# A two-layer trunk on one core: weights in 8 KB pieces, evenly spaced row passes, attention on the full array

## The chip, the core and the metric

The kernel runs on one core of a Trainium2 chip. The core has TensorE (PE in the profile, PEld its weight loads), VectorE (DVE), ScalarE (ACT), GpSimd (POOL) and SyncE (SP); here SP only issues DMAs, and 16 DMA engines move the data from the chip's memory into the core's. The metric is the time of one execution on the device in microseconds (us). The clock that TensorE is granted has two levels, 1.2 and 2.4 GHz; the profile gives it as a share of the higher.

## What is computed

One sequence of 256 positions with 1024 features goes through two layers, all in float32. Each layer is a half-weighted SwiGLU, a mixer and another half-weighted SwiGLU; every one of the six has its own RMSNorm, shift, scale and gate, which come from the conditioning vector c by a matrix `mod_w` of 1024 x 9216 for each layer. The mixer of layer 0 is half a gated MLP over chunks of 128 positions, half a stick-breaking attention with 8 heads of 64; that of layer 1 is a short causal convolution.

```python
def stick_breaking_attention(q, k, v):          # A[t,s] = beta[t,s] * prod_{s<j<t} (1 - beta[t,j]), s < t
    for blk in range(S // Q_BLOCK):
        ...
        z = jnp.einsum('bqhd,bkhd->bhqk', qb, kb) * scale
        before = s_pos < t_pos
        log_1mb = jnp.where(before, -jax.nn.softplus(z), 0.0)
        tail = lax.cumsum(log_1mb, axis=3, reverse=True) - log_1mb
        w = jnp.where(before, jnp.exp(jax.nn.log_sigmoid(z) + tail), 0.0)
        outs.append(jnp.einsum('bhqk,bkhd->bqhd', w, v[:, :kv_len]))
...
for layer in range(DEPTH):
    mod = cond @ mod_w[layer] + mod_b[layer]      # nine vectors: shift, scale, gate of three sub-layers
    h = modulate(x, norm_g[layer, 0], sh1, sc1)
    x = x + 0.5 * g1 * swiglu(h, ffn_w_gate[layer, 0], ffn_w_up[layer, 0], ffn_w_down[layer, 0])
    h = modulate(x, norm_g[layer, 1], sh2, sc2)
    x = x + g2 * (gmlp_stickbreak_mixer(h, ...) if layer % 2 == 0 else short_conv_mixer(h, ...))
    h = modulate(x, norm_g[layer, 2], sh3, sc3)
    x = x + 0.5 * g3 * swiglu(h, ffn_w_gate[layer, 1], ffn_w_up[layer, 1], ffn_w_down[layer, 1])
return rms_norm(x, final_norm_g)
```

## The kernel before

**Products.** Activations lie with features on the 128 partitions and the 256 positions along the free axis. A float32 product is made of three float32r products (`mm3`, L473): high half of the weight by high half of the activation, high by low, low by high. In the names `hh` and `hl` are the halves of a normalised activation, `ah` and `al` those of an inner one, `h_g` and `l_g` those of a weight tile of 128x1024. The attention's small products stay float32, which PE does in two passes; the profile shows each as two records.

**Weights.** A unit is 1 MB (`colunit` L289, 256 columns of a matrix; `rowunit` L292, 256 rows; `rows4` L768). `load` (L295) issues its DMA on SP. A column unit is read as pieces of 1 KB, `rows4` as 2 KB, a row unit as 4 KB. ACT casts a half unit to the high half (`split_hi` L338, by `cp`, L216) and DVE subtracts that from the weight for the low half (`split_lo` L353, L176).

**Row passes.** Each of the 18 vectors is 8 steps (`mod_step` L406): one pass of DVE (L199) over a 128x1024 piece of `mw`, multiplied by the conditioning and summed. Beside the 16 that the start makes in another way there are 128 of them. A load of 1 MB (`mod_load` L385) serves two steps, and there are two buffers for it. `can_mod` (L400) allows a step when its piece has been loaded; nothing else holds it back.

**What sets the order.** The program is written out in Python while a planner (`Pace`, `clk`) keeps a clock for each engine from costs noted with each call (for a float32r product of n columns n/2.26 + 6 ns). `pump` (L453) runs between groups of products: it issues loads that have a buffer, casts and subtractions that are due, and a row pass where DVE's clock stands 800 ns behind PE's. `fill_dve` (L147) puts subtractions and row passes into time in which DVE would wait by the planner. `defer` (L440) puts a step off to a time, `run_deferred` (L446) issues what is due, and `mod_need` (L432) makes the steps of a vector that is now needed. So an engine's instructions are in a fixed order, and each waits by semaphore for its inputs.

**The stages.** FFN, hybrid mixer, FFN, FFN, convolution, FFN, final norm. In an FFN, gate and up products of two tiles of 256 columns alternate (tile `pf`, 96 products) with the down products (`pd`, 48 at a time). A sub-layer is entered with raw products (`proj_entry` L581, tile `pe`) whose normalisation follows at the eviction; their operand needs the residual `xT`, which `down_last` (L617) updates on DVE from `pd`, or `pdc` behind the convolution.

**The attention.** `hybrid` (L783) projects q and k of heads 0 to 3 (`ps0`, evicted by `first_qk` L822), then q and k of heads 4 to 7, then the gated MLP's v. `vb` and the gated MLP's `uu` are filler (`fills` L886, tiles `pvb` and `pu`), of which `fill` takes a number at each step. For head h `scores` (L910) makes three 128x128 blocks of z over the 64 rows where the head's q and k lie; `chain` does |z|, exp and ln on ACT, `softplus` (L925) one DVE instruction, and `diag` (L906) sets the masked part to zero by an affine select on POOL (`keep_if` L232). `tails` (L932) adds the sums of sp over later positions to z with the triangle `negtri` and the all-ones `neg1`; `weights` (L941) is the exponential on ACT and a second select; `values` (L948) multiplies by vb into 64 rows of `py`, two heads to a bank, which ACT and DVE split into `yh` and `yl`. The loop (L1015) runs 11 times: scores of head i, filler, tails of head i-2, gating (`pg`, L977) at two of them, from the eighth on four steps of the output projection (`pdh`) instead of filler, and values of head i-3.

## Time and profile before

| what | value |
|---|---|
| device time, median of 3 runs | 987.56 us (985.64 to 988.4) |
| the profiled execution, its own time | 984.59 us |
| its span | 982.9 us |
| PE busy | 969.8 us, 99% |
| DVE busy | 757.4 us, 77% |
| ACT busy | 483.9 us, 49% |
| POOL busy | 18.2 us, 2% |
| read from memory | 247.32 MB, 253 GB/s over the span |

The span goes from the first to the last instruction of the profiled execution; 1.7 us of its own time lie around it. "Busy" is the sum of the times in which an engine had work. An average over the program says little of a stage: DMA is at 254 GB/s over the span, but its busy share by slices of 24.6 us goes from 0 to 9 tenths, so the stages are to be read one by one. A busy PE is not one that can't be relieved either, and the clock that it was granted belongs beside it. In a timeline a row's duration runs on to the end of the last of its instructions and overlaps the next row; what a group costs is read from start to start.

### The profile page before, as it was taken

Reading aid. Unit: us, or ns where it says so; the run is one execution under the profiler, and the core shown is the slowest. Engines: PE = TensorE matmul, PEld = TensorE weight load, DVE = VectorE, ACT = ScalarE, POOL = GpSimd, SP = SyncE. Lnnn points to the kernel's source line nnn. Section 1 sums busy time; section 2 is a strip of 40 time slices with the busy share of each in tenths; the row PEclk is TensorE's granted clock in tenths of the full one; section 3 lists DMA queues with packets and bytes.
Section 4 is the critical chain, followed back from the end, with each engine's and each line's share of the span. In section 5 each row is a group of like instructions: output and inputs, shape, how many; then the busy total and the mean of one; then the engine's idle time right before and its main releaser. Section 6 shows DMA issues by size and latency. Waiting matters only on the chain.

```text
span 982.9 us, 18893 instructions
## 1 busy us (share of the span) xinstructions
PE 969.8 (99%) x7948; PEld 956.4 (97%) x7948; DVE 757.4 (77%) x1124; ACT 483.9 (49%) x678; POOL 18.2 (2%) x27
## 2 busy tenths in 40 slices
PE   8999999999999999999999999999999999999997
PEld 7999999998789999999989999999999999999997
DVE  7997888898979978787899787864986796544432
ACT  4465344365667644344365443444644565534333
POOL 0000000000410000000000000000000000000000
PEclk9999999999999999999999999999999999999999
DMA  9998999849885598988976898666258438465401
GB/s 350 405 321 301 387 340 360 321 175 312 280 270 174 171 382 284 386 307 312 327 256 206 308 365 305 243 244 215 79 196 271 142 112 283 163 215 172 171 2 43
DMA packets 142261, 249.59 MB, mean 254 GB/s; under 512 B 4320, under 2 KB 105568, under 8 KB 142176
## 3 DMA queue, kind: packets, MB, share of 16 engines
q1 hardware_dynamic: 142176, 248.39, 71.8%
q8 instruction: 62, 1.02, 0.4%
q14 instruction: 23, 0.19, 0.1%
HBM read 247.32 MB, written 1.05 MB: 253 GB/s over the span
## 4 chain that ended last, share of the span: by engine, by line
PE 81%; DVE 8%; DMA 8%; issue 2%; ACT 1%; SPq 0%; POOL 0%; DVEq 0%
PE pf L139 38%; PE pd L139 20%; DMA mw<-in_mod_w_dram 5%; PE pe L139 4%; PE ps L139 4%; PE pc L139 3%; PE pdh L139 2%; PE pdc L139 2%; PE pcb L139 2%; DVE mw L199 2%; PE pec L139 1%; DMA w_s<-in_ffn_w_gate_dram 1%; PE pu L139 1%; PE z L139 1%; DMA mws<-in_mod_w_dram 1%
## 5 line engine op out<-in xcount | busy, mean ns | idle before, releaser
L199 DVE CUSTOM_DVE_ANT_0 mw<-mw,cond,cols_sb 128x1024 f32<-128x1024 f32 x128 | 164.9, 1307 | 52.2 <-DMA mw<-in_mod_w_dram 52.1
L139 PE MATMUL pd<-ah,l_d 128*128 128x256 f32 x704 | 198.2, 282 | 0.0
L139 PE MATMUL pd<-al,h_d 128*128 128x256 f32 x704 | 198.1, 281 | 0.0
L139 PE MATMUL pd<-ah,h_d 128*128 128x256 f32 x704 | 198.1, 281 | 0.0
L139 PE MATMUL pf<-hh,h_u 128*128 128x256 f32 x592 | 167.3, 283 | 0.0
L139 PE MATMUL pf<-hl,h_u 128*128 128x256 f32 x592 | 166.7, 282 | 0.0
L139 PE MATMUL pf<-hh,l_g 128*128 128x256 f32 x592 | 166.6, 281 | 0.0
L139 PE MATMUL pf<-hh,l_u 128*128 128x256 f32 x592 | 166.5, 281 | 0.0
L139 PE MATMUL pf<-hh,h_g 128*128 128x256 f32 x592 | 166.4, 281 | 0.0
L139 PE MATMUL pf<-hl,h_g 128*128 128x256 f32 x592 | 166.4, 281 | 0.0
L216 ACT CAST h_g<-w_g 128x1024 fp32r<-128x1024 f32 x80 | 83.9, 1049 | 107.1 <-issue 79.1
L216 ACT CAST h_d<-w_d 128x1024 fp32r<-128x1024 f32 x88 | 88.4, 1048 | 94.8 <-PE pf L139 72.9
L176 DVE TENSOR_TENSOR l_d<-w_d,h_d 128x1024 fp32r<-128x1024 f32 x88 | 104.2, 1219 | 37.8 <-ACT h_d L216 37.8
L139 PEld LDWEIGHTS pd<-al,h_d 128*128 128x128 f32 x704 | 132.7, 189 | 0.0
L139 PEld LDWEIGHTS pd<-ah,h_d 128*128 128x128 f32 x704 | 132.7, 188 | 0.0
L139 PEld LDWEIGHTS pd<-ah,l_d 128*128 128x128 f32 x704 | 132.6, 188 | 0.0
L176 DVE TENSOR_TENSOR l_g<-w_g,h_g 128x1024 fp32r<-128x1024 f32 x80 | 97.6, 1220 | 29.4 <-ACT h_g L216 29.3
L139 PEld LDWEIGHTS pf<-hl,h_u 128*128 128x128 f32 x592 | 112.0, 189 | 0.0
L139 PEld LDWEIGHTS pf<-hh,l_u 128*128 128x128 f32 x592 | 111.9, 189 | 0.0
L139 PEld LDWEIGHTS pf<-hh,l_g 128*128 128x128 f32 x592 | 111.8, 189 | 0.0
L139 PEld LDWEIGHTS pf<-hh,h_u 128*128 128x128 f32 x592 | 111.8, 189 | 0.0
L139 PEld LDWEIGHTS pf<-hh,h_g 128*128 128x128 f32 x592 | 111.8, 189 | 0.0
(298 smaller groups left out, 1877.6 us busy)
## 6 DMA issues: line engine op xcount, KB each, us to landing
mw<-in_mod_w_dram SPq DMA_DIRECT2D x64, 1024.0 KB, 8.3
w_d<-in_ffn_w_down_dram SPq DMA_DIRECT2D x44, 1024.0 KB, 7.0
w_g<-in_ffn_w_gate_dram SPq DMA_DIRECT2D x40, 1024.0 KB, 7.5
w_u<-in_ffn_w_up_dram SPq DMA_DIRECT2D x40, 1024.0 KB, 5.5
mws<-in_mod_w_dram SPq DMA_DIRECT2D x14, 512.0 KB, 10.1
w_s<-in_ffn_w_gate_dram SPq DMA_DIRECT2D x8, 512.0 KB, 10.2
w_s<-in_ffn_w_up_dram SPq DMA_DIRECT2D x8, 512.0 KB, 10.2
w_ho<-in_hy_w_out_dram SPq DMA_DIRECT2D x4, 1024.0 KB, 8.7
```

Source lines behind the costliest of these rows:

```text
L139: return nc.tensor.matmul(out=out_, lhsT=lhsT, rhs=rhs, start=start, stop=stop, skip_group_check=True)
L176: nc.vector.tensor_tensor(out=out_, in0=a, in1=b, op=op)
L199: nc.vector.tensor_tensor_reduce(out=src, in0=src, in1=cond, scale=scale, scalar=init, op0=ALU.mult, op1=ALU.add, accum_out=dst)
L216: nc.scalar.copy(out=out_, in_=in_)
```

## The change

**Weights.** The matrices are handed over in another layout, so that each 1 MB unit is 128 pieces of 8 KB, one for a partition; the start's units stay in 4 KB pieces, from one tensor instead of two.

**Row passes.** The first 50 steps are free as before. Step n after them is allowed only when the planner's clock of PE has come to 300 us + 6 us x (n - 50). `mod_need` loads a piece that isn't there.

**Attention.** k is held in two copies, in each of which the rows of the other head are zero (four POOL memsets), so that z is made over 128 rows. The mask becomes a product: `hide` (-2^100 where a position is masked) times the identity, both float32r, is added to z in PSUM, and the selects on POOL go. sp is split into float32r halves, `sh` by a cast on ACT and `sl` by a subtraction on DVE, and the tails are four float32r products instead of two float32 ones. Values multiply by the vb of both heads of a pair, 128 columns, into a half of `py` for each head, of which the valid 64 rows are kept, in two instructions each. w is written over sp. v and vb are loaded ahead of q and k of heads 4 to 7, whose projections become filler. The loop's order is values, gating, scores, tails, filler; the output projection begins at the ninth step.

```diff
+HIDE = -2.0 ** 100
+MOD_FREE, MOD_FROM, MOD_EACH = 50, 300000.0, 6000.0
...
+    ident_r = const.tile([P, P], F32R, name="ident_r")
+    nc.gpsimd.tensor_copy(out=ident_r, in_=ident)
+    hide = const.tile([P, 2 * P], F32R, name="hide")
+    veil = new(lop, "lo", "veil", HALF, (P, 1024), F32R).bitcast(F32)[:, 0:2 * P]
+    nc.gpsimd.memset(veil, HIDE)
+    keep_if(veil.rearrange("p (b t) -> p b t", b=2), [[0, 2], [-1, P]], ALU.is_ge, 1)
+    nc.gpsimd.tensor_copy(out=hide, in_=veil)
...
     def colunit(w, c0, name):
-        return add_unit(name, [(0, 2048, 8, w[:, c0:c0 + 256].rearrange("(k p) n -> p k n", p=P))])
+        return add_unit(name, [(0, 2048, None, w[c0 // 256].rearrange("p k n -> p (k n)"))])
     def rowunit(w, r0, name):
-        return add_unit(name, [(0, 2048, 2, w[r0:r0 + 256, :].rearrange("(k p) n -> p k n", p=P))])
+        return add_unit(name, [(0, 2048, None, w[r0 // 256].rearrange("p k n -> p (k n)"))])
...
     def can_mod():
-        return mq["step"] // 2 < len(mod_loaded)
+        n = mq["step"]
+        return n // 2 < len(mod_loaded) and (n < MOD_FREE or MOD_FROM + MOD_EACH * (n - MOD_FREE) <= clk.pe)
...
     def mod_need(l, v):
         while mq["step"] < 8 * (mod_units.index((l, v)) + 1):
+            while mq["step"] // 2 >= len(mod_loaded):
+                mod_load()
             mod_step()
...
         add_halves(colunit(w_in, 1024, "q0"), colunit(w_in, 1536, "k0"))
-        add_halves(colunit(w_in, 1280, "q1"))
-        add_halves(colunit(w_in, 1792, "k1"))
         for c0, name in ((512, "v"), (2048, "vb")):
             for part in range(2):
                 add_halves(rows4(c0, part, f"{name}{part}"))
+        add_halves(colunit(w_in, 1280, "q1"))
+        add_halves(colunit(w_in, 1792, "k1"))
...
+        kT1 = [new(work, "al", f"kT1{k}", 4, (P, 2, S), F32R).bitcast(F32) for k in range(2)]
+        kTs = [[kT[:, 2 * k:2 * k + 2, :] for k in range(2)], kT1]
+        heads = [slice(64 * e, 64 * e + 64) for e in range(2)]
+        for e in range(2):
+            for k in range(2):
+                zeros = kTs[e][k][heads[1 - e]]
+                nc.gpsimd.memset(zeros, 0.0)
+                clk.op("pool", 600.0, [], [zeros])
...
-                ts(kT[:, j, :], u, col[:, 0:1], None, ALU.add)
+                for e in range(2):
+                    ts(kTs[e][0][heads[e], j, :], u[heads[e]], col[heads[e], 0:1], None, ALU.add)
...
-        psq = dbank("pq1")
-        run(proj_t(psq, 4))
-        defer(clk.pe, lambda: act(qT[:, 2:4, :], psq.rearrange("p (j s) -> p j s", j=2), AF.Copy,
-                                  scale=HD ** -0.5))
-        psk = dbank("pk1")
-        run(proj_t(psk, 4))
-        defer(clk.pe, lambda: cp(kT[:, 2:4, :], psk.rearrange("p (j s) -> p j s", j=2)))
...
+            psq = dbank("pq1")
+            yield from proj_t(psq, 2)
+            defer(clk.pe, lambda: act(qT[:, 2:4, :], psq.rearrange("p (j s) -> p j s", j=2), AF.Copy,
+                                      scale=HD ** -0.5))
+            psk = dbank("pk1")
+            yield from proj_t(psk, 2)
+            def second_k():
+                for e in range(2):
+                    cp(kTs[e][1][heads[e]], psk[heads[e]].rearrange("p (j s) -> p j s", j=2))
+            defer(clk.pe, second_k)
...
-        def diag(t):
-            tv = t[:, 0:256].rearrange("p (b t) -> p b t", b=2)
-            keep_if(tv, [[0, 2], [1, P]], ALU.is_gt)
         def scores(h):
             z = gbank(f"z{h}")
-            r0 = 64 * (h % 2)
-            qs = qT[r0:r0 + 64, h // 2, :]
-            ks = kT[r0:r0 + 64, h // 2, :]
+            qs = qT[:, h // 2, :]
+            ks = kTs[h % 2][h // 4][:, h // 2 % 2, :]
             for i, (s, t) in enumerate(((0, 0), (1, 1), (0, 1))):
-                mm(z[:, i * P:(i + 1) * P], ks[:, s * P:(s + 1) * P], qs[:, t * P:(t + 1) * P], i == 0, True)
+                mm(z[:, i * P:(i + 1) * P], ks[:, s * P:(s + 1) * P], qs[:, t * P:(t + 1) * P], i == 0, i == 2)
+            mm(z[:, 0:2 * P], ident_r, hide, False, True)
             zz = z[:, 0:384]
             sp = new(work, "e1", f"sp{h}", 4, (P, 384))
...
                 defer(act(sp, sp, AF.Ln, bias=1.0), softplus)
             def softplus():
-                stt(sp, zz, 0.0, sp, ALU.max, ALU.add)
-                diag(sp)
-                zs[h] = (z, sp)
+                defer(stt(sp, zz, 0.0, sp, ALU.max, ALU.add), halves)
+            def halves():
+                sh = new(work, "sq", f"sh{h}", 2, (P, 384), F32R)
+                def rest():
+                    sl = new(work, "sl", f"sl{h}", 2, (P, 384), F32R)
+                    tt(sl, sp, sh.bitcast(F32), ALU.subtract)
+                    zs[h] = (z, sp, sh, sl)
+                defer(cp(sh, sp), rest)
             defer(clk.pe, chain)
         def tails(h):
             while h not in zs:
                 run_deferred(True)
-            z, sp = zs.pop(h)
+            z, sp, sh, sl = zs.pop(h)
             zz = z[:, 0:384]
-            mm(zz, negtri, sp, False, False)
-            mm(z[:, 256:384], neg1, sp[:, 128:256], False, True)
-            w = new(work, "ah", f"w{h}", 4, (P, 384), F32R).bitcast(F32)
+            for part in (sh, sl):
+                mm(zz, negtri, part, False, False)
+                mm(z[:, 256:384], neg1, part[:, 128:256], False, part is sl)
+            w = sp
             def weights():
                 act(w, zz, AF.Exp)
-                diag(w)
                 ws[h] = w
             defer(clk.pe, weights)
...
             while h not in ws:
                 run_deferred(True)
             w = ws.pop(h)
-            hp, r0 = h // 2, 64 * (h % 2)
+            hp, c0 = h // 2, S * (h % 2)
             if h % 2 == 0:
                 pys[hp] = (dbank if hp < 2 else gbank)(f"py{hp}")
             py = pys[hp]
             for i, (s, t, src) in enumerate(((0, 0, 0), (0, 1, 2), (1, 1, 1))):
-                mm(py[r0:r0 + 64, t * P:(t + 1) * P], vb[:, s, h * HD:(h + 1) * HD], w[:, src * P:(src + 1) * P],
+                mm(py[:, c0 + t * P:c0 + (t + 1) * P], vb[:, s, hp * P:(hp + 1) * P], w[:, src * P:(src + 1) * P],
                    i == 0, i == 2)
...
+        def beside(n):
+            if out_b is None:
+                fill(n)
+            else:
+                for _ in range(5 * n // 2):
+                    next(out_b, None)
         for i in range(11):
+            if i == 8:
+                run(filler)
+                run_deferred(True)
+                banks += [dbank(f"pdh_{b}") for b in range(4)]
+                out_b = down_steps(banks, lambda: yb[0], True)
+            if i == 4:
+                beside(1)
+                run_deferred(True)
+            if 0 <= i - 3 < 8:
+                values(i - 3)
+            if i in (5, 6):
+                gating(i - 5)
             if i < 8:
                 scores(i)
-            fill((3, 3, 2, 1, 2, 1, 2, 1, 1, 1, 1)[i])
             if 0 <= i - 2 < 8:
                 tails(i - 2)
             if i == 9:
                 defer(clk.pe, gelu_u)
-            if i in (5, 6):
-                gating(i - 5)
-            if i >= 7:
-                if i == 7:
-                    run(filler)
-                    run_deferred(True)
-                    banks += [dbank(f"pdh_{b}") for b in range(4)]
-                    out_b = down_steps(banks, lambda: yb[0], True)
-                for _ in range(4):
-                    next(out_b, None)
-            if 0 <= i - 3 < 8:
-                values(i - 3)
+            beside((4, 5, 4, 3, 1, 2, 2, 2, 2, 2, 2)[i])
...
+    def columns(w):
+        w = np.reshape(w, (*w.shape[:-2], NC, P, -1, 256))
+        return np.moveaxis(w, -2, -4).swapaxes(-3, -2)
+    def units_of_rows(w):
+        return np.reshape(w, (*w.shape[:-2], -1, 2, P, D)).swapaxes(-3, -2)
```

The first place is PE's order for one head in the attention. Before:

```order
L139 MATMUL pu_3042<-hh_2423,l_uu_0_2888 128x256
L139 MATMUL z_2960<-sp_2964,negtri 128x384
L139 MATMUL z_2960<-sp_2964,neg_102 128x128
L139 MATMUL py_3073<-w_3036,vb 64x128 x3
L139 MATMUL z_3077<-qT,kT 128x128 x3
L139 MATMUL pu_3042<-hh_2423,h_uu_0_2865 128x256
L139 MATMUL pu_3042<-hl_2424,h_uu_0_2865 128x256
L139 MATMUL pu_3042<-hh_2423,l_uu_0_2888 128x256
```

After (`pu` is filler, `neg_102` the all-ones tile, `x3` three in a row; the line numbers differ by the added lines):

```order
L144 MATMUL py_3020<-sp_2862,vb 128x128 x3
L144 MATMUL z_3115<-qT,kT 128x128 x3
L144 MATMUL z_3115<-hide,ident_r 128x256
L144 MATMUL z_2932<-sh_2965,negtri 128x384
L144 MATMUL z_2932<-sh_2965,neg_102 128x128
L144 MATMUL z_2932<-sl_2975,negtri 128x384
L144 MATMUL z_2932<-sl_2975,neg_102 128x128
L144 MATMUL pu_3093<-hh_2432,h_uu_0_2889 128x256
```

Two tail products of one head, then values and scores, have become values, scores and the mask's product, then four tail products, with sh and sl in the place of sp.

The second is ACT's order in the attention, near head 4, before:

```order
L211 ACTIVATE sp_3081<-z_3077 128x384
L211 ACTIVATE sp_3081<-sp_3081 128x384 x2
L216 CAST h_ho_1_3105<-w_ho_2869 128x1024
L211 ACTIVATE w_3122<-z_3004 128x384
L216 CAST yh_3126<-py_3073 128x256
L211 ACTIVATE sp_3132<-z_3128 128x384
L211 ACTIVATE sp_3132<-sp_3132 128x384 x2
```

and after:

```order
L221 CAST yh_3113<-py_3020 64x256 x2
L216 ACTIVATE sp_3120<-z_3115 128x384
L216 ACTIVATE sp_3120<-sp_3120 128x384 x2
L216 ACTIVATE sp_2937<-z_2932 128x384
L221 CAST h_ho_1_3150<-w_ho_2903 128x1024
L221 CAST sh_3181<-sp_3120 128x384
L216 ACTIVATE sp_3170<-z_3165 128x384
L216 ACTIVATE sp_3170<-sp_3170 128x384 x2
```

Between the two activations of one head and the exponential for w of another (w before, written into sp after) the cast `sh` has come in, and it stands behind a weight cast.

The third is DVE's order just ahead of the first residual update at the entry of layer 1, before (L199 is a row pass, its second row reads the sum):

```order
L199 ISA mw_5586,mod_5662<-mw_5586,cond,cols_sb 128x1024
L199 ISA mod_5662 128x1
L176 TENSOR_TENSOR l_u_1_0_5769<-w_u_1_5571,h_u_1_0_5736 128x1024
L199 ISA mw_5646,mod_5662<-mw_5646,cond,cols_sb 128x1024
L199 ISA mod_5662 128x1
L176 TENSOR_TENSOR l_g_1_1_5798<-w_g_1_5524,h_g_1_1_5767 128x1024
L199 ISA mw_5646,mod_5662<-mw_5646,cond,cols_sb 128x1024
L199 ISA mod_5662 128x1
L176 TENSOR_TENSOR hl_5803<-mod_4079,hh_5802 128x8x2
L187 SCALAR_TENSOR_TENSOR xT<-pd_0_4084,mod_3272,xT 128x256 x2
```

and after:

```order
L181 TENSOR_TENSOR l_g_1_0_5760<-w_g_1_5549,h_g_1_0_5727 128x1024
L204 ISA mw_5582,mod_5774<-mw_5582,cond,cols_sb 128x1024
L204 ISA mod_5774 128x1
L181 TENSOR_TENSOR l_u_1_0_5790<-w_u_1_5598,h_u_1_0_5758 128x1024
L204 ISA mw_5582,mod_5774<-mw_5582,cond,cols_sb 128x1024
L204 ISA mod_5774 128x1
L181 TENSOR_TENSOR l_g_1_1_5821<-w_g_1_5549,h_g_1_1_5788 128x1024
L181 TENSOR_TENSOR hl_5826<-mod_4415,hh_5825 128x8x2
L192 SCALAR_TENSOR_TENSOR xT<-pd_0_4129,mod_3590,xT 128x256 x2
```

Here three passes among the last weight subtractions have become two. Counted in the whole order, 100 of the 128 passes stand ahead of this update before and 82 after (55 and 49 by the end of the hybrid mixer); 128 and 113 by the end of the next FFN, 128 and 123 by the end of the convolution, and five in the last FFN.

## Rows read from the trace of the kernel before

**Rows 1.** The page: span, engines, and granted clock in 40 slices (tenths).
```profile
span 982.9 us, 18893 instructions
...
PE 969.8 (99%) x7948; PEld 956.4 (97%) x7948; DVE 757.4 (77%) x1124; ACT 483.9 (49%) x678; POOL 18.2 (2%) x27
...
PEclk9999999999999999999999999999999999999999
```

**Rows 2.** The chain of waits, second FFN: start, us, engine and line.
```profile
367.74 11.43 PE pf L139 x96
379.17 5.69 PE pd L139 x48
```

**Rows 3.** All waits of PE, 30 to 975: us in total, times, longest.
```profile
PE pe L139 <- ACT hh L221: 2.1, 1, 2.1
PE py L139 <- POOL w L234: 1.3, 1, 1.3
```

**Rows 4.** Windows at two entries: length, busy (count), granted clock, DMA share, GB/s.
```profile
498.80:510.20 11.40, 9.21 (x61) 0.85 0.59 232
784.20:795.60 11.40, 11.40 (x96) 1.00 0.32 93
```

**Rows 5.** Waits of DVE for mw, 415 to 500, columns as in rows 3.
```profile
DVE mw L199 <- DMA mw<-in_mod_w_dram: 13.1, 6, 3.7
```

**Rows 6.** Timeline of DVE and PE at both entries: start, us; idle before in brackets.
```profile
487.30 1.28 DVE L199 CUSTOM_DVE_ANT_0 mw<-mw,cond,cols_sb 128x1024 f32<-128x1024 f32 x1 [3.68 <-DMA mw<-in_mod_w_dram]
...
499.15 0.87 DVE L187 SCALAR_TENSOR_TENSOR xT<-pd,mod,xT 128x256 f32<-128x256 f32 x2
...
779.96 0.88 DVE L187 SCALAR_TENSOR_TENSOR xT<-pdc,mod,xT 128x256 f32<-128x256 f32 x2
...
498.80 0.28 PE L139 MATMUL pd<-ah,l_d 128*128 128x256 f32 x1
501.14 0.38 PE L139 MATMUL pe<-hh,h_g 128*128 128x258 f32 x1 [2.06 <-ACT hh L221]
...
784.06 0.28 PE L139 MATMUL pe<-hh,h_g 128*128 128x258 f32 x1
```

**Rows 7.** Windows, all engines, start and second FFN; DMA share and GB/s last.
```profile
25.00:50.00 25.00, 24.66 (x203) 24.24 (x203) 23.79 (x35) 12.27 (x15) 0.00 (x0) 1.00 1.03 403
...
425.00:450.00 25.00, 25.00 (x212) 25.00 (x211) 21.44 (x30) 10.69 (x15) 0.00 (x0) 1.00 1.05 376
```

**Rows 8.** Timeline of PE in the attention, a head and the gating.
```profile
263.45 0.81 PE L139 MATMUL z<-sp,negtri 128*128 128x384 f32 x2
264.10 0.38 PE L139 MATMUL z<-sp,neg 128*128 128x128 f32 x2
264.41 0.87 PE L139 MATMUL py<-w,vb 128*64 128x128 f32 x6
265.21 0.93 PE L139 MATMUL z<-qT,kT 64*128 64x128 f32 x6
266.07 0.38 PE L139 MATMUL pu<-hh,h_uu 128*128 128x256 f32 x1
266.29 0.28 PE L139 MATMUL pu<-hl,h_uu 128*128 128x256 f32 x1
...
268.56 1.15 PE L139 MATMUL pg<-wsT,v 128*64 128x128 f32 x16
269.48 0.38 PE L139 MATMUL py<-w,vb 128*64 128x128 f32 x2
```

**Rows 9.** Timeline of POOL, the select that the first py waited for.
```profile
257.40 1.39 POOL L234 TENSOR_SCALAR_AFFINE_SELECT w<-w 128x256 f32<-128x256 f32 x1
```

**Rows 10.** Timeline of ACT and DVE in the attention: activations, a cast, the softplus.
```profile
260.67 0.49 ACT L211 ACTIVATE sp<-z 128x384 f32<-128x384 f32 x1 [1.31 <-PE z L139]
261.19 1.08 ACT L211 ACTIVATE sp<-sp 128x384 f32<-128x384 f32 x2
...
265.32 0.37 ACT L216 CAST yh<-py 128x256 fp32r<-128x256 f32 x1 [0.31 <-PE py L139]
...
262.36 0.56 DVE L187 SCALAR_TENSOR_TENSOR sp<-z,sp 128x384 f32<-128x384 f32 x1 [0.77 <-POOL w L234]
```

**Rows 11.** Windows of DVE around the convolution: busy (count), granted clock, DMA share, GB/s.
```profile
725.00:750.00 25.00, 20.15 (x32) 1.00 0.77 262
...
sum 125.00, DVE 100.81; mean DVE 20.16
```

**Rows 12.** The costliest wait of DVE, 675 to 800.
```profile
DVE l_g L176 <- ACT h_g L216: 7.1, 2, 3.7
```

More of the change, by code (lines that the diff above doesn't have):

```diff
@@ L88, in trunk @@
 @with_exitstack
[L89 to L90 removed]
+def trunk(ctx: ExitStack, tc: tile.TileContext, x, c, mod_w, cols, start_gu,
+          ffn_w_gate, ffn_w_up, ffn_w_down, hy_w_in, hy_w_v, hy_w_out,
           gm_w_s, gm_b_s, sc_w_in, sc_w_out, out):
@@ L260, in trunk @@
     nc.gpsimd.memset(mean_w, 1.0 / D)
-    neg1 = const.tile([P, P], F32, name="neg1")
-    nc.gpsimd.memset(neg1, -1.0)
-    negtri = const.tile([P, P], F32, name="negtri")
-    nc.gpsimd.memset(negtri, -1.0)
-    keep_if(negtri, [[-1, P]], ALU.is_ge, 1)
+    neg1 = const.tile([P, P], F32R, name="neg1")
+    negtri = const.tile([P, P], F32R, name="negtri")
+    minus = new(lop, "lo", "minus", HALF, (P, 1024), F32R).bitcast(F32)[:, 0:P]
+    nc.gpsimd.memset(minus, -1.0)
+    nc.gpsimd.tensor_copy(out=neg1, in_=minus)
+    keep_if(minus, [[-1, P]], ALU.is_ge, 1)
+    nc.gpsimd.tensor_copy(out=negtri, in_=minus)
+    ident_r = const.tile([P, P], F32R, name="ident_r")
[5 more added lines that the diff above has]
+    nc.gpsimd.tensor_copy(out=hide, in_=veil)
     cond = const.tile([P, D], F32, name="cond")
@@ L966, in keep @@
                 def keep():
-                    defer(cp(ah[:, hp % 2, :], py[:, 0:S]), keep_lo)
+                    for e in range(2):
+                        t_h = cp(ah[heads[e], hp % 2, :], py[heads[e], e * S:(e + 1) * S])
+                    defer(t_h, keep_lo)
                 def keep_lo():
-                    tt(al[:, hp % 2, :], py[:, 0:S], ah[:, hp % 2, :].bitcast(F32), ALU.subtract)
+                    for e in range(2):
+                        tt(al[heads[e], hp % 2, :], py[heads[e], e * S:(e + 1) * S],
+                           ah[heads[e], hp % 2, :].bitcast(F32), ALU.subtract)
                 defer(clk.pe, keep)
@@ L1156, in trunk @@
     ncol = NS * 256
-    start_units = [add_unit(f"s{dc}", [(i * ncol, ncol, None, w[0, 0, dc * P:(dc + 1) * P, 0:ncol])
-                                       for i, w in enumerate((ffn_w_gate, ffn_w_up))], ncol) for dc in range(NC)]
+    start_units = [add_unit(f"s{dc}", [(i * ncol, ncol, None, start_gu[dc, :, i]) for i in range(2)], ncol)
+                   for dc in range(NC)]
     for u in start_units:
@@ L1384, in rows @@
         return [np.reshape(i[n], (-1, P)) for n in names]
+    def columns(w):
[3 more added lines that the diff above has]
+        return np.reshape(w, (*w.shape[:-2], -1, 2, P, D)).swapaxes(-3, -2)
+    start = [np.reshape(i[n][0, 0][:, :NS * 256], (NC, P, NS * 256)) for n in ("ffn_w_gate", "ffn_w_up")]
+    hy_v = [np.reshape(i["hy_w_in"][0][:, c0:c0 + 512], (2, 4, P, 512)).swapaxes(1, 2) for c0 in (512, 2048)]
     return {
@@ L1390, in _laid_out @@
         "cols": np.concatenate(rows("norm_g", "final_norm_g", "sc_conv_w", "gm_vnorm_g", "mod_b")).T,
-        "ffn_w_gate": i["ffn_w_gate"], "ffn_w_up": i["ffn_w_up"], "ffn_w_down": i["ffn_w_down"],
-        "hy_w_in": i["hy_w_in"], "hy_w_out": i["hy_w_out"],
+        "start_gu": np.stack(start, axis=2),
+        "ffn_w_gate": columns(i["ffn_w_gate"]), "ffn_w_up": columns(i["ffn_w_up"]),
+        "ffn_w_down": units_of_rows(i["ffn_w_down"]),
+        "hy_w_in": columns(i["hy_w_in"]), "hy_w_v": np.stack(hy_v), "hy_w_out": units_of_rows(i["hy_w_out"]),
         "gm_w_s": np.transpose(i["gm_w_s"][0], (2, 0, 1)),
-        "gm_b_s": i["gm_b_s"], "sc_w_in": i["sc_w_in"], "sc_w_out": i["sc_w_out"],
+        "gm_b_s": i["gm_b_s"], "sc_w_in": columns(i["sc_w_in"]), "sc_w_out": units_of_rows(i["sc_w_out"]),
     }
```

5 lines of the change are left out of this document (1 added, 4 removed).

## Prediction

> **What bounds the kernel now.** The page first: PE is busy for 969.8 of 982.9 us, and the clock it is granted stands at the top in every slice [rows 1]. The chain of waits then shows what a busy PE is worth: 96 products in 11.43 us and 48 in 5.69, so 0.119 us for each 128x256 float32r product [rows 2]. Pieces of DVE and of mw's transfers stand in that chain too, but a chain shows what came last, not what was lost; the waits of PE decide. After the start it waits twice: 2.1 us for the first gate product of layer 1 (tile pe) and 1.3 us for the first py [rows 3]. So only three things can shorten the program: these two waits, what hangs on them, and fewer or cheaper products on PE.
>
> The first wait is dearer than 2.1 us. After the last pd of layer 0 (498.80) there are 61 products in 11.40 us at a mean clock of 0.85; the same entry one sub-layer later, at 784.20, does 96 at 1.00 [rows 4]. PE stood idle, was then granted the lower level for some products, and lost (96 - 61) x 0.119 = 4.2 us. DVE is why it stood: its first residual updates (xT) start at 499.15, after PE's last product, while at the later entry they start at 779.96, four us ahead of PE's first pe at 784.06 [rows 6]. DVE is late because it had stood 13.1 us in six waits for mw, 3.68 of it at 487.30, and had these row passes still ahead of the xT updates [rows 5, 6]. The transfers are late because the DMA engines are full: 1.05 of their time for 376 GB/s in 425 to 450; at the start, where a piece is 4 KB, 1.03 gave 403 [rows 7].
>
> **The change part by part.**
>
> *Pieces of 8 KB and evenly spaced row passes.* These belong together: both end at the entry of layer 1. The period there is 11.43 + 5.69 = 17.1 us [rows 2]. By the order, five row passes in a period become three, so 3 + 2.5 = 5.5 units of 1 MB become 3 + 1.5 = 4.5, 276 instead of 337 GB/s at 1.049 MB each. Against the 358 that a full share gave with small pieces (376/1.05) the share falls from 0.94 to 0.77; with pieces at least as good as those of the start (403/1.03 = 391) to 0.71 [rows 7]. The first would do by itself; the second adds room. In the order 12 row passes fewer stand ahead of this entry in the second FFN, 12 x 1.28 [rows 6] = 15.4 us of DVE, against the 13.1 it waited plus the few us by which it was late. I take the whole 4.2 us; bounds 2.1 (something else keeps half) to 4.2.
>
> The passes go elsewhere: three more beside the next FFN, ten more beside the convolution, five in the last FFN. Beside the convolution (675 to 800) DVE is busy for 100.81 of 125 us [rows 11]; ten times 1.28 is 12.8 of the 24.2 that are idle. Two queues are passed: SP issues mw between the weights, and a transfer into a buffer that DVE still reads would hold the weights behind it. With the passes later, the transfer is due later too, and the DMA share there, 0.77 at most, is below that of the second FFN [rows 7, 11]. I cost it at nothing; if the cover is gone, the price is an entry like that at 498.80 again, 4.2 us at the convolution's end.
>
> *No selects on POOL.* Sixteen selects go. One took 1.39 [rows 9], and the 1.3 us for py end with w's. Gain 1.3; bounds 0 (another wait stands there) to 1.3. POOL's new set-up (fills, casts) lies ahead of the attention, where POOL does nothing else; I cost it at nothing, and if q0's or k0's eviction had to wait for a fill of kT, the slack of the first scores below is what it would eat.
>
> *The head itself.* Eight heads stand in rows like 263.45 to 266.29 [rows 8]: tails 0.96 (fp32 negtri 0.65, neg1 0.31), py 0.80, z 0.86, and 0.22 instead of 0.12 for the first pu behind; 2.84 - 0.12 = 2.72 us beside the filler. The fp32 passes go at 0.65/768 columns, 0.108 for 128 columns; so of py's and z's six, 0.15 and 0.21 are changes between the halves of the array. After: z on all 128 rows, 0.65 to 0.86; py on all columns, 0.65 to 0.80; one hide product, 0.12; tails of four float32r products, where 384 columns are 0.18 (96 give 11.43, by columns) and 128 columns lie between 0.06 (by columns) and 0.11 (one fp32 pass of that width), 0.48 to 0.58; and up to 0.22 for changes of type. Ends 1.90 and 2.58, gain 0.82 to 0.14, eight times: 6.6 to 1.1. I take z at 0.85 with its change, py at 0.65, hide 0.12, tails 0.53: 2.15, since full-array rows followed each other with no gap (z on negtri straight after pu at 263.45). Gain 8 x 0.57 = 4.6 us.
>
> A rule speaks against the full array. In the rows a head's six 64-row passes take 0.86 and start in one piece; only pg's sixteen show two halves at work together, 0.92 for sixteen, 0.057 each [rows 8]. The Trainium skill (TensorE: Matmul & The Clock Gate, Why this matters for your kernels) says that products over fewer than 128 rows run at the same time if they lie in distinct row groups. Zero-padded scores give that up: if z of two heads were interleaved at 0.057, a head would have cost 0.34 instead of 0.65, and 8 x 0.31 = 2.5 us are not to be had. The kernel before doesn't interleave heads, so nothing is lost by its rows. The same page (Back-to-back issue gap) gives an N=128 pair some 81 ns; the two narrow tails would be 0.16 by that, tails 0.52, within my ends.
>
> *New waits.* The masks now come before the softplus, and sp is split: a cast on ACT and a subtraction on DVE stand between softplus and tails. Chain before: 0.49 + 1.08 on ACT, 0.56 on DVE, 1.39 on POOL; after: the same without POOL, then a cast of some 0.5 (0.37 for 256 columns) and 0.56 [rows 9, 10]. It is 0.3 us shorter, and tails still come two heads behind. But w's exponential is queued on ACT behind the next head's two activations (1.6 us), and py waits for w. Between them PE has 24 filler products in most steps (2.86 us) and 12 at the fifth (1.43, with tails 0.5). So one wait of 0.5 to 1; DVE can put a row pass (1.28) ahead of one subtraction. Estimate 0.8; bounds 0 to 3. The first scores: q1 and k1, 5.7 us each of PE, become filler behind them, so z comes sooner after q0 and k0; two more evictions on DVE (about 0.35 each, half of a 256-column row) stand in front, and I find about 1.4 us to spare. Changing the filler's order moves no product in or out.
>
> **Sum.** -4.2 - 1.3 - 4.6 + 0.8 = -9.3 us. Span 982.9 to 973.6, the profiled run 984.59 to 975.3; the median of the runs stands 3.0 above that run: 978.3 us.
>
> **Rivals.**
> A, *the attention gives its gain back*: ACT carries one cast more for each head, DVE one subtraction, and the selects' work didn't bother PE except once. If PE now waits 0.6 to 0.8 for each head, heads and POOL's wait together bring nothing: -4.2, 983.4. For it: a planner places these queues by its own costs, and the 12-product steps are thin. Against: before, PE waited once in eight heads, with a longer chain.
> B, *the change doesn't relieve the entry*: DVE stays late at 499, or becomes late at the convolution's end with ten passes more. Then -1.3 - 4.6 + 0.8 = -5.1, 982.5. For it: DVE's costliest wait between 675 and 800 is for ACT's casts, 7.1 us of the 24.2 for one tile, and such time comes back only if the planner sets passes there [rows 12]. Against: the idle 24.2 us, and the xT updates there have 4 us to spare [rows 6].
> C, *slower, by ACT's queue in the attention*: sh's cast waits on ACT for DVE's softplus, and the exponential of the head before and the weight casts (1.05) are queued behind it; py and with it PE wait for both. With one cast and a softplus activation in front, about 2.0 us for each head, it is 16 instead of 0.8: +5.9, 993.5. It decides from 10.1/8 = 1.3 us of waiting per head on. Against it: ACT is issued in the planner's order, where the cast is put behind the softplus's due time and not ahead of it.
> The idle array may also be granted the lower clock level, as at 502; in A and C that is in the price.
>
> **How the numbers follow.** Forecast 0.74: 978.3, own range from -12.1 (heads 6.6, no new wait) less 0.9 for a median's spread, 974.5, to heads near 2.2 and the same spread, 981.6. A 0.12, B 0.09, C 0.05. The range reaches to 984.5, which takes in A and B with their spread; C and some ends of the others, about 0.12, are left out. Within 0.3% of before, which is what a measurement of this kernel can tell from no change, ends at 984.6. Faster: 0.74, B nearly whole and half of A, 0.87. The same: the rest of A and B, 0.08. Slower: C, 0.05.
>
> **What would show it.** In the changed kernel's profile: no wait of pe for hh at the entry of layer 1, some 96 products in the first 11.4 us there at clock 1.00, xT updates starting before PE's last pd; few and short DVE waits for mw; a DMA share near 0.7 in the second FFN. In the attention: 2.1 to 2.2 us of PE for a head, no POOL, and less than a us of waits of py or z for ACT or DVE. At the convolution's end the xT updates still ahead of pe. I am wrong if z and py cost more on the full array than their passes (heads' gain near 1), if the waits there sum to more than 3 us, or if the entry's 4.2 us appear again at another entry.

## The result and the profile after

The changed kernel takes 973.83 us (median of 4 runs, 973.71 to 974.38); the kernel before took 987.98 beside it (985.64 to 988.72). The ratio is 0.9862, interval 0.9845 to 0.9879: 14 us, or 1.4%, faster. The forecast was 978.3 with a range from 974.5, so the direction was right and the size wrong: 9.3 us were expected, and the time lies 0.7 us below the range.

The page of the kernel after, to be read beside [rows 1]:

```profile
span 971.9 us, 18915 instructions
...
PE 962.0 (99%) x7956; PEld 954.9 (98%) x7956; DVE 764.4 (79%) x1138; ACT 490.5 (50%) x691; POOL 11.0 (1%) x20
...
PEclk9999999999999999999999999999999999999999
```

From profile to profile the span fell by 11.0 us. Both waits of PE in [rows 3] are gone; the view of PE's waits has no row between 30 and 965. The windows at the entry of layer 1, in the second FFN, and at the entry behind the convolution (length, busy and count of PE, PEld, DVE, ACT, POOL, granted clock, DMA share, GB/s; the last one PE alone), beside [rows 4, 7]:

```profile
488.63:500.03 11.40, 11.40 (x96) 11.35 (x95) 10.78 (x23) 9.98 (x18) 0.00 (x0) 1.00 0.32 115
425.00:450.00 25.00, 25.00 (x213) 25.00 (x212) 18.48 (x23) 10.44 (x15) 0.00 (x0) 1.00 0.65 237
...
773.20:784.60 11.40, 11.40 (x96) 1.00 0.27 93
```

The entry of layer 1 has its 96 products at the full clock, and the DMA engines have a third of their time left. DVE's timeline ahead of that entry, beside [rows 6], where the last brackets name PE and ACT in the place of the DMA:

```profile
483.46 1.28 DVE L204 CUSTOM_DVE_ANT_0 mw<-mw,cond,cols_sb 128x1024 f32<-128x1024 f32 x1
...
487.77 0.18 DVE L181 TENSOR_TENSOR hl<-mod,hh 128x16 fp32r<-128x16 f32 x1 [1.75 <-ACT hh L221]
488.12 0.88 DVE L192 SCALAR_TENSOR_TENSOR xT<-pd,mod,xT 128x256 f32<-128x256 f32 x2 [0.18 <-PE pd L144]
```

DVE now waits for PE's products there, not PE for DVE. The ten passes that went beside the convolution show nowhere in PE's time.

One head of the attention, PE's timeline, beside [rows 8]:

```profile
272.38 0.83 PE L144 MATMUL py<-sp,vb 128*128 128x128 f32 x6
273.05 0.83 PE L144 MATMUL z<-qT,kT 128*128 128x128 f32 x6
273.64 0.36 PE L144 MATMUL z<-hide,ident_r 128*128 128x256 f32 x1
273.84 0.34 PE L144 MATMUL z<-sh,negtri 128*128 128x384 f32 x1
274.02 0.22 PE L144 MATMUL z<-sh,neg 128*128 128x128 f32 x1
274.08 0.39 PE L144 MATMUL z<-sl,negtri 128*128 128x384 f32 x1
274.30 0.22 PE L144 MATMUL z<-sl,neg 128*128 128x128 f32 x1
274.36 0.34 PE L144 MATMUL pu<-hh,h_uu 128*128 128x256 f32 x1
274.53 0.28 PE L144 MATMUL pu<-hl,h_uu 128*128 128x256 f32 x1
```

From start to start: py 0.67, z 0.59, hide 0.20, tails 0.52, and 0.05 more than its usual 0.12 for the first pu. That is 2.03 us for a head, where [rows 8] had 2.72. From the two traces the 11 us are: 4.2 at the entry of layer 1, 6.6 in the attention (from the first product of the hybrid mixer to that of the second FFN 98.93 us, before 105.54), 0.1 ahead of both. The 6.6 are 8 x 0.69 = 5.5, the wait for py with 1.4 by its starts, and 0.26 lost again at another py. (The expectations below say 6.7, which counts in the 0.1.)

### The profile page after: what moved, and what is told of

It reads as the page before. It is cut to its first block, busy times and chain, and to the rows that moved or that the text cites. A ratio compares the mean times of both kernels' runs of the same rounds, so it can differ in the third digit from the quotient of the medians.

```text
span 971.9 us, 18915 instructions
## 1 busy us (share of the span) xinstructions
PE 962.0 (99%) x7956; PEld 954.9 (98%) x7956; DVE 764.4 (79%) x1138; ACT 490.5 (50%) x691; POOL 11.0 (1%) x20
## 4 chain that ended last, share of the span: by engine, by line
PE 96%; DMA 2%; ACT 0%; SPq 0%; DVE 0%; issue 0%; DVEq 0%
PE pf L144 44%; PE pd L144 26%; PE ps L144 4%; PE pe L144 4%; PE pc L144 4%; PE pdh L144 2%; PE pdc L144 2%; PE pcb L144 2%; PE pec L144 1%; PE peh L144 1%; DMA w_s<-in_start_gu_dram 1%; PE pvb L144 1%; PE pv L144 1%; PE z L144 1%; PE pu L144 1%; DMA mws<-in_mod_w_dram 1%
## 5 line engine op out<-in xcount | busy, mean ns | idle before, releaser
L221 ACT CAST h_u<-w_u 128x1024 fp32r<-128x1024 f32 x80 | 83.8, 1048 | 55.8 <-PE pd L144 31.6
```

The lines of the kernel that those rows point to most:

```text
L221: nc.scalar.copy(out=out_, in_=in_)
```

## The experiments

Theory D, formed on the result: what the entry of layer 1 loses is DVE being late because mw's transfers are late, and the 3 us by which the runs of before lie over its profiled run are the same loss in another size. Theory M: the attention gained because PE no longer changes between halves of the array, not because of fewer passes. The rivals are in the expectations; "before" is the kernel before, run beside them (medians 988.55 beside the first four, 988.4 beside the next four, 987.51 beside the last four).

### Each part alone

Weights in 8 KB pieces alone:

```diff
     def rowunit(w, r0, name):
-        return add_unit(name, [(0, 2048, 2, w[r0:r0 + 256, :].rearrange("(k p) n -> p k n", p=P))])
+        return add_unit(name, [(0, 2048, None, w[r0 // 256].rearrange("p k n -> p (k n)"))])
...
```

> The kernel before with the weights in 8 KB pieces alone. Theory D: the loss at the entry of layer 1 (4.2 us in the profile) and the 3 us by which the median of before stands over its profiled run are both DVE waiting for mw while the DMA engines are full. Then larger pieces alone give the DMA room: share in 425 to 450 under 0.95, DVE's waits for mw in 415 to 500 under 5 us, no wait of pe, median 980 to 982. Rival P: the row passes' rate is the cause, pieces change nothing: the entry's 2.1 us wait and lower clock stay, median 986 to 988. Rival Q: the 3 us are not of this entry: median 983 to 984, and runs still spread over 2 us.

982.93 us (981.3 to 985.79), ratio 0.9947 (0.9932 to 0.9961). The window 415 to 500 and DVE's waits for mw in it (us, times, longest) show half a cure:

```profile
415.00:500.00 85.00, 84.45 (x709) 84.13 (x707) 71.14 (x98) 36.06 (x49) 0.00 (x0) 1.00 0.86 324
```

```profile
DVE mw L202 <- DMA mw<-in_mod_w_dram: 13.8, 5, 4.2
```

In the same window of before 321 GB/s took a share of 0.90:

```profile
415.00:500.00 85.00, 84.08 (x707) 83.88 (x706) 70.50 (x96) 34.35 (x44) 0.00 (x0) 1.00 0.90 321
```

So 8 KB give 377 GB/s for a full share, the smaller pieces 357: 6% more. But DVE waits no less for mw than the 13.1 us of [rows 5], since the passes go as fast as the data comes; pe waits 0.5 us in the profile, and the runs spread over 4 us. P's "nothing" is wrong. The entry's loss shrinks as D had it, but D's "waits under 5 us", its share (0.97 in 425 to 450, not under 0.95) and its median are missed, and the median and the spread lie nearer to Q's 983 to 984 and "over 2 us": this run doesn't decide between D and Q.

Spaced row passes alone:

```diff
     def can_mod():
-        return mq["step"] // 2 < len(mod_loaded)
+        n = mq["step"]
+        return n // 2 < len(mod_loaded) and (n < MOD_FREE or MOD_FROM + MOD_EACH * (n - MOD_FREE) <= clk.pe)
...
```

> The kernel before with the evenly spaced row passes alone, pieces and attention as before. Theory D: share in the second FFN 0.75 to 0.85, no wait of pe, clock 1.00 at the entry; median 980 to 982, spread of the runs under 1 us. Rival Q (the 3 us of the median come from elsewhere, say the selects): entry as in D, but median 983 to 984 with a spread over 2 us. Rival B of the prediction: the wait comes back at the convolution's end, 986 to 988.

981.59 us, ratio 0.9939 (0.9917 to 0.9961); five runs from 980.39 to 982.32 and one of 988.58, and the profile is of that one. D had the median, the share (0.75 in 425 to 450) and the entry of layer 1, but not the spread (under 1 us). Its trace tells why: the entry of layer 1 is clean and the loss stands elsewhere. PE's waits:

```profile
PE peh L140 <- ACT hh L222: 3.0, 1, 3.0
PE py L140 <- POOL w L235: 2.1, 1, 2.1
```

The first is the entry of the hybrid mixer, where the first 50 passes aren't held back; ahead of it DVE had waited up to 6.2 us for mw. The second is the select of w, and here PE was granted the lower level behind it; the window from there on (PE alone):

```profile
263.80:275.20 11.40, 11.24 (x59) 0.70 0.73 237
```

In the profiled run of before that wait was 1.3 us [rows 3] and cost its own length; this one of 2.1 cost the clock as well. The longer wait at peh did not; the window from there on (PE alone):

```profile
207.30:218.70 11.40, 11.13 (x86) 1.00 0.43 154
```

So where mw is late, any of three places can pay, in a run more or less.

The attention alone (all of its edits, pieces and passes as before):

```diff
-                stt(sp, zz, 0.0, sp, ALU.max, ALU.add)
-                diag(sp)
-                zs[h] = (z, sp)
+                defer(stt(sp, zz, 0.0, sp, ALU.max, ALU.add), halves)
...
```

> The kernel before with the attention's changes alone. By the trace of the changed kernel the time between the entry of the hybrid mixer and that of the second FFN falls by 6.7 us. Theory D: the entry of layer 1 keeps a loss of about 4 us (94 passes stand ahead of it, 100 before), so median 980 to 982 and runs that spread over 2 us. Rival Q: the selects made the spread; spread under 1 us, median 977 to 978.

981.11 us (979.71 to 983.74), ratio 0.9927 (0.9913 to 0.994). The profile has no wait for POOL and a wait of pe of 3.3 us: D and not Q.

Pieces and passes without the attention:

```diff
+MOD_FREE, MOD_FROM, MOD_EACH = 50, 300000.0, 6000.0
...
-        return add_unit(name, [(0, 2048, 2, w[r0:r0 + 256, :].rearrange("(k p) n -> p k n", p=P))])
+        return add_unit(name, [(0, 2048, None, w[r0 // 256].rearrange("p k n -> p (k n)"))])
...
```

> The kernel before with pieces of 8 KB and spaced row passes, attention as before. If the parts add up, the attention is 6.7 us of the trace and this is 980 to 981, spread under 2 us, with one wait of py for POOL. Rival: the attention's change also helps at the entries (six passes and 7 us moved), then 982 or more.

980.31 us (979.59 to 981.84), ratio 0.9915 (0.9889 to 0.9941): 6.5 above the changed kernel. The parts add up; the spread is 2.3, not under 2. The wait of py is still there:

```profile
PE py L143 <- POOL w L238: 0.8, 1, 0.8
```

### One part taken back

The changed kernel with the old pieces:

```diff
-        return add_unit(name, [(0, 2048, None, w[r0 // 256].rearrange("p k n -> p (k n)"))])
+        return add_unit(name, [(0, 2048, 2, w[r0:r0 + 256, :].rearrange("(k p) n -> p k n", p=P))])
...
```

> The changed kernel with the weights in their pieces of 1, 2 and 4 KB again; pacing and attention stay. If pacing alone gives the DMA enough room (share near 0.8 in the second FFN), the time is that of the changed kernel, 973.5 to 974.5. Rival: the pieces carry part of it, a wait for mw or weights stands at an entry: 976 to 979, or a spread over 2 us.

973.93 us (973.61 to 974.61), ratio 0.9853 (0.984 to 0.9865). The DMA share in 425 to 450, the last number but one here, is 0.67 (0.65 in the changed kernel), lower than the 0.8 that was expected:

```profile
425.00:450.00 25.00, 25.00 (x213) 25.00 (x212) 18.48 (x23) 10.55 (x15) 0.00 (x0) 1.00 0.67 239
```

Once the passes are spaced, the pieces carry nothing that the time shows.

The changed kernel without the spacing:

```diff
-        return n // 2 < len(mod_loaded) and (n < MOD_FREE or MOD_FROM + MOD_EACH * (n - MOD_FREE) <= clk.pe)
+        return n // 2 < len(mod_loaded)
...
```

> The changed kernel with row passes that aren't held back: pieces of 8 KB and attention stay. With pieces alone the entry of layer 1 waited 0.5 us, with 13.8 us of DVE waiting for mw ahead of it. If pieces are half a cure there, this is 974.5 to 978 with a spread over 1.5 us and a wait of pe in the profile; if the attention's shift of six passes out of the way makes it whole, 973.5 to 974.5.

979.06 us (974.81 to 981.59), ratio 0.9903 (0.9885 to 0.9921): 5 us lost, more than expected, and a spread of 7. Its entry of layer 1, PE alone:

```profile
492.30:503.70 11.40, 8.49 (x57) 0.85 0.70 258
```

### Is it the transfers or the passes?

The order is that of before; from the 25th pass on, half of each mw unit is loaded:

```diff
-        nc.sync.dma_start(out=raw, in_=mod_w[l, v, 2 * part:2 * part + 2].rearrange("c p k -> p c k"))
+        if i < 12:
+            nc.sync.dma_start(out=raw, in_=mod_w[l, v, 2 * part:2 * part + 2].rearrange("c p k -> p c k"))
+        else:
+            nc.sync.dma_start(out=raw[:, 0, :], in_=mod_w[l, v, 2 * part])
...
-        dot_v(mod_loaded[n // 2][0][:, n % 2, :], mod_cols[(l, v)][:, chunk:chunk + 1], scale,
+        dot_v(mod_loaded[n // 2][0][:, n % 2 if n < 24 else 0, :], mod_cols[(l, v)][:, chunk:chunk + 1], scale,
```

> The kernel before with every instruction of DVE, ACT and PE in its place, but from the 25th row pass on only half of each mw unit is loaded and both passes go over that half (so half of the modulation's weights are left out). Theory D: DVE is late at the entry of layer 1 because mw's transfers are late. With 0.5 MB instead of 1 MB for two passes they aren't: no wait of pe, DVE's waits for mw under 4 us in 415 to 500, median 981 to 982.5 as with pacing alone. Rival V: DVE has too many passes to do there, however early the data; the loss stays, 987 to 989.

980.92 us (980.52 to 981.69), ratio 0.9922 (0.9896 to 0.9947), 0.1 below the 981 that D gave, and no row left among PE's waits nor among DVE's for mw in 415 to 500. The same passes stand in the same places, and every engine's instructions are in the order of before, so V falls and D is shown: late transfers, not too many passes. The spread falls as well, to 1.2 us, where the kernel before, run beside it, went from 984.95 to 993.7. From issue to landing the twelve loads of mw in 415 to 500, now half as large, take 5.7 us (median), in before 8.7. What makes them late is less sure: the window's DMA share falls to 0.72 from 0.90 (first line), but in before mw's loads also wait on SP until DVE has freed one of the two buffers (second line, us, times, longest):

```profile
415.00:500.00 85.00, 85.00 (x717) 85.00 (x716) 73.95 (x103) 39.30 (x53) 0.00 (x0) 1.00 0.72 250
SPq L391 <- DVE mod L199: 20.1, 11, 4.4
```

A third buffer was not tried, so full engines and too few buffers are not told apart.

The wait of py for the select is gone too, with the selects on POOL as before. So that wait was not POOL's alone. In the profile of before DVE waits for mw ahead of it, and its later softplus holds the selects up:

```profile
246.11 1.34 DVE L199 CUSTOM_DVE_ANT_0 mw<-mw,cond,cols_sb 128x1024 f32<-128x1024 f32 x1 [3.81 <-DMA mw<-in_mod_w_dram]
```

With halved loads that wait is 2.6 us, and PE no longer stops. Pieces and spacing don't reach it, since the pass is one of the first 50: py still waits 1.2 us with pieces alone and 0.8 with both.

### A usual run of before

The kernel before, unchanged.

> The kernel before, unchanged, for a trace of one of its usual runs (11 in the last job took 987.6 to 989.7, the profiled one on which the prediction rests 984.6). Theory S: the 3 us between them are the wait of py for the select of w, longer here (2 us or more) and followed by products at the lower clock, as in the run of pacing alone that took 988.6; the entry of layer 1 loses 4 to 5 us as before. Rival E: they are at an entry of a sub-layer (a wait of peh for hh, 3 us), with py's wait near 1.3 and no fall of the clock.

988.77 us. PE's waits, and the window at the entry of layer 1 (PE alone):

```profile
PE pe L139 <- ACT hh L221: 3.1, 1, 3.1
PE py L139 <- POOL w L234: 1.4, 1, 1.4
PE pd L139 <- DVE al L176: 0.7, 1, 0.7
PE pd L139 <- ACT ah L216: 0.4, 1, 0.4
```

```profile
501.93:513.33 11.40, 8.14 (x53) 0.85 0.66 255
```

Neither S nor E. Of the 4.2 us over the profiled run 1.4 are at the start, by the windows 28 to 61 (PE alone) of this run and of the profiled one:

```profile
28.00:61.00 33.00, 32.96 (x264) 0.95 0.99 368
28.00:61.00 33.00, 32.98 (x276) 1.00 0.99 367
```

The rest is the same entry again: pd stops twice ahead of it, 1.6 us by its starts, and then come 53 products in 11.40 us instead of 61, 8 x 0.119 = 1.0. In this run the entry loses 43 x 0.119 + 1.6 = 6.7 us, not 4.2. The 1.4 at the start have nothing to do with the change: a run of the changed kernel with z on half the rows (below) has 264 products at 0.95 there too. So what D said of the 3 us holds for about two thirds of the difference in this run.

### The attention's parts

z over the head's own 64 rows, all else as changed:

```diff
-            qs = qT[:, h // 2, :]
-            ks = kTs[h % 2][h // 4][:, h // 2 % 2, :]
+            qs = qT[heads[h % 2], h // 2, :]
+            ks = kTs[h % 2][h // 4][heads[h % 2], h // 2 % 2, :]
```

> The changed kernel with z made over the head's own 64 rows again (mask product, tails and values stay on the full array). Theory M: what the full array saves is the change between the halves of the array, about 0.38 us around z in the rows of before (0.09 + 0.10 ahead, 0.09 + 0.10 behind): 8 x 0.2 to 0.38, 975.4 to 976.9. Rival: rows don't matter, only the number of passes: 973.8.

976.81 us (976.5 to 977.99), ratio 0.9881 (0.9867 to 0.9896): 3.0 slower. PE's timeline of one head:

```profile
276.24 0.83 PE L144 MATMUL py<-sp,vb 128*128 128x128 f32 x6
277.00 0.93 PE L144 MATMUL z<-qT,kT 64*128 64x128 f32 x6
277.86 0.39 PE L144 MATMUL z<-hide,ident_r 128*128 128x256 f32 x1
278.08 0.34 PE L144 MATMUL z<-sh,negtri 128*128 128x384 f32 x1
```

The same six passes take 0.86 instead of 0.59, py ahead of them 0.76 instead of 0.67, and hide 0.22 instead of 0.20: 0.38 for a head, 8 x 0.38 = 3.0. Single starts show where: from the second on the 64-row passes follow each other 0.11 us apart, as on the full array, and the extra lies before the first, before the second and around the start of hide. So M holds at its upper end. In the profile the stretch from the hybrid mixer's first product to the second FFN's grows by 2.7, from 98.93 to 101.61. The rule weighed in the prediction, that small-K products side by side would be cheaper (the Trainium skill, TensorE: Matmul & The Clock Gate, Why this matters for your kernels), was not tried with heads interleaved (the 0.057 that the prediction took from pg are halves by columns, not by rows); for one head at a time the run shows the 64 rows dearer by these changes. That a change of mode costs something at all is also stated (the Trainium skill, TensorEngine Tiling (Array Packing), Key Properties: TensorE drains when the tiling mode changes); the size, 0.1 us and more on each side, is this trace's.

Tails as two float32 products, without sh and sl:

```diff
...
-            for part in (sh, sl):
-                mm(zz, negtri, part, False, False)
-                mm(z[:, 256:384], neg1, part[:, 128:256], False, part is sl)
+            mm(zz, negtri, sp, False, False)
+            mm(z[:, 256:384], neg1, sp[:, 128:256], False, True)
```

> The changed kernel with two float32 tail products of sp for each head, no sh and sl. Passes alone: 0.65 + 0.22 to 0.31 instead of 0.17 + 0.06 + 0.23 + 0.06 = 0.52, so 8 x 0.35 to 0.44 = 2.8 to 3.5 slower, 976.6 to 977.3. Rival: the chain through sh and sl costs waits that this saves, and the time stays within 1 us, 973 to 974.8.

975.99 us (975.84 to 976.09), ratio 0.9874 (0.9861 to 0.9887): 2.2 slower, a little under the expectation by passes: with the excess of the first filler a head's tails take 0.86 instead of 0.57, 8 x 0.29 = 2.3, and most of the 0.26 us that py loses in the changed kernel aren't lost here. The split of sp pays, though it adds a cast and a subtraction.

Selects on POOL instead of the mask's product:

```diff
...
-            mm(z[:, 0:2 * P], ident_r, hide, False, True)
...
-                defer(stt(sp, zz, 0.0, sp, ALU.max, ALU.add), halves)
+                stt(sp, zz, 0.0, sp, ALU.max, ALU.add)
+                diag(sp)
+                defer(clk.pool, halves)
...
                 act(w, zz, AF.Exp)
+                diag(w)
```

> The changed kernel with the two selects of each head on POOL again and no mask product; all else on the full array. Theory W: the product costs PE 8 x 0.20 = 1.6 us, but POOL's selects (0.4 to 1.45 each) in the two chains make PE wait for w or sl once or more, 1.3 us and up: 973 to 975.5, with a wait for POOL in the profile. Rival N: the new order hides the selects, and 1.6 us come off: 972.0 to 972.6.

977.89 us (977.35 to 979.12), ratio 0.9893 (0.9867 to 0.9919): 4.1 slower, more than W. PE's waits, and the window behind the longest one (PE alone):

```profile
PE py L144 <- POOL sp L239: 3.3, 3, 1.7
```

```profile
281.00:290.00 9.00, 7.28 (x48) 0.81 0.66 241
```

In this run, the slowest of the six, 3.3 us are waited, and the lower clock after the wait of 1.7 costs another 1.6 by the starts. What is saved is less than the 1.6 expected, as one head's rows show:

```profile
273.67 0.83 PE L144 MATMUL z<-qT,kT 128*128 128x128 f32 x6
274.26 0.42 PE L144 MATMUL z<-sh,negtri 128*128 128x384 f32 x1
274.52 0.22 PE L144 MATMUL z<-sh,neg 128*128 128x128 f32 x1
```

Without hide the first tail behind z takes 0.26 instead of 0.17, so the mask's product costs a head 0.11, not the 0.20 from its start to the next: 0.9 in all. The mask's product is the cheaper way, in this order.

The cast to sh made twice:

```diff
+                cp(sh, sp)
                 defer(cp(sh, sp), rest)
```

> The changed kernel with the cast to sh made twice, 0.5 us more of ACT's queue for each head. If ACT has room everywhere but at the fifth step (0.26 us of waiting there), 0.5 us are lost once: 974.1 to 974.6. By the prediction's rival C, with ACT's queue near its limit in each head, 8 x 0.5: 976.5 to 978.

976.1 us (975.86 to 976.38), ratio 0.9873 (0.9844 to 0.9901): 2.3 slower, but neither way. py's lost 0.26 us are as they were, and no head waits. The planner, with ACT's clock further on, set three row passes in a row ahead of the updates of xT at the mixer's end, where the changed kernel has one. PE's wait there, and DVE's timeline:

```profile
PE pe L144 <- ACT hh L226: 0.9, 1, 0.9
```

```profile
299.65 1.34 DVE L204 CUSTOM_DVE_ANT_0 mw<-mw,cond,cols_sb 128x1024 f32<-128x1024 f32 x1
...
300.92 1.34 DVE L204 CUSTOM_DVE_ANT_0 mw<-mw,cond,cols_sb 128x1024 f32<-128x1024 f32 x1
...
302.38 1.27 DVE L192 SCALAR_TENSOR_TENSOR xT<-pdh,mod,xT 128x256 f32<-128x256 f32 x3
```

The changed kernel's first xT update there starts at 299.62. So 2.6 us of passes in front of an entry cost 2.3 us of time, 2.0 of them between 303 and 312 by the starts of PE's products: the margin at this entry is small. How near ACT's queue is to its limit within the heads stays open beyond 0.5 us a head.

## Why the prediction was wrong

- **The entry of layer 1, -4.2.** Right against the profiled run: 96 products at clock 1.00, xT updates waiting for PE. Of the cause it named, halving the loads shows that the transfers come late; that full DMA engines make them late is argued from the share. That share came out at 0.65 in 425 to 450, for 0.71, since fewer bytes were moved (237 GB/s, not 276). The page's "top in every slice" was read too far: a 9 is 90% or more, and in 491.4 to 516 of before the clock is 0.93.
- **The step that failed first: "the median of the runs stands 3.0 above that run".** The sum was made on the profiled execution and the 3.0 us were then added unchanged. But the profiled run of before was quicker than every other run of it (984.95 to 993.7), and a good part of what varies between its runs is the very loss that the change removes: 6.7 us in the usual run that was traced, 4.2 in the profiled one; another 1.4 of that run's 4.2 were at its start. After the change the runs lie within 0.7 us and the median 0.06 over the profiled run. This is 2.9 of the 4.5 us by which the forecast missed. The 3.0 stood in both ends of the range too, so the range had no room for this.
- **The step that failed second: "z at 0.85 with its change".** On the full array z and the mask's product together take 0.59 + 0.20 = 0.79, for 0.85 + 0.12 = 0.97. The run with selects gives the mask's product 0.11, as forecast, which leaves 0.68 for z, near the low end of the bounds given (0.65). The prediction had itself read 0.21 of z's 0.86 as a change between halves, and then left it in, although behind the change no halves are used by z and py. It is 0.17 x 8 = 1.4 us too little. Tails were right (0.52 for 0.53; by starts the two narrow ones take 0.06 each, not the 81 ns that the prediction cited beside its ends, and the sum is the same), py nearly (0.67 for 0.65), and the first filler's 0.05 was put at nothing. Heads: 5.5 for 4.6.
- **New waits, +0.8.** 0.26, at the step with 12 filler products, as placed, so 0.5 too much. Rival C didn't appear, and half a microsecond more of ACT per head brought no wait there either.
- **POOL's wait, -1.3.** Right in size, but its cause was only half read: a late transfer of mw stood behind it. The pieces and the passes alone leave 0.8 of it; the run with selects in the new order shows that there they would have cost far more than they did before.
- **Rival B and the moved passes.** The convolution took the ten passes for nothing, as costed. The entry whose margin is thin is another, at the end of the hybrid mixer.
- **The pieces.** Said to add room; they do (6% in 415 to 500), and the time doesn't show it with the passes spaced.

The sum by its own steps with the right sizes is -4.2 - 1.4 - 5.5 + 0.3 = -10.8, and the profiled run went from 984.59 to 973.77, 10.8. That the direction came out is no luck; that the profiled run of before was a quick one made the change look smaller than it is.

## What to carry to other kernels

A wait that depends on transfers at the edge of their rate differs from run to run: before it is priced from one profile, look at how the runs spread and where the profiled one lies among them. Here removing the wait removed most of the spread, and the median fell by more than the profile showed. Background work that shares DMA or an engine with the main stream should be set to the rate it needs over the whole program, not done as early as it can be. Where small products use part of PE's array between full ones, price the changes on both sides apart from the passes.

## What the runs showed of the hardware

Going from the full array to 64 rows and back for one group of six small passes costs 0.38 us, of which 0.09 lie ahead of the group; inside it the passes go at 0.11 us like those on the full array. A product's time from its start to the next one's is not always its price: hide showed 0.20 and cost 0.11.

Waits of PE of 2.1 us (at pe in before, at py with passes spaced alone), of 2.9 to 3.3 (at pe in three other traces) and of 1.7 (at py with selects) were followed by products at the lower of the two clock levels. After waits of 1.3 and 1.4 at py the clock stayed at the upper one, but so it did after the 3.0 at peh with passes spaced alone: the wait's length by itself didn't tell. Nor did it at the start, where PE waits 1.3 to 1.7 us at ps in most traces: two of these waits, of 1.5 and 1.6, were followed by the lower level, one of 1.7 was not.

Pieces of 8 KB instead of 1 to 4 KB gave 6% more bytes for the same busy share in 415 to 500, 377 against 357 GB/s; in 425 to 450 of the two kernels with spaced passes the difference was 2% (237/0.65 = 365 against 239/0.67 = 357). Of small transfers the Trainium skill (DMA: Bandwidth & Descriptors, Specifications) says that line rate needs 512 B; between 1 and 8 KB these windows still show that difference.
